# Four tiles and the samples gather first, and the last four tiles are dense

## The chip, the core and the metric

The kernel runs on one core of one Trainium2 chip. The metric is the device time in microseconds (us) of one execution. The version before takes 3297.21 us (median of 3 runs, 3287.35 to 3303.12).

## The reference

One layer of a decoder trunk is computed for a prompt of 1024 positions (eight tiles of 128) and for eight samples of four positions (32 rows, called the samples, tile NT = 8 in the code). Both use the same weights.

```python
ada = silu(c) @ W_ada + b_ada                    # shift, scale, gate, twice
y   = token_mixers(x * (1 + sc1) + sh1)          # mLSTM, spatial gating, pooling, then @ W_o
x   = LN(ALPHA * x + g1 * y)
q   = (x * (1 + sc2) + sh2) @ W_pq               # PEER: 8 heads, two halves of 128
s   = q . keys                                   # 128 keys a half; top 16 of each half
idx, g = top 16 of the 256 sums of both halves, softmax
act = gelu(x2 . peer_u[idx]); out = sum(g * act * peer_v[idx])
x   = LN(ALPHA * x + g2 * out)
```

Each position so picks 8 x 16 = 128 of 16384 experts. Each expert has a row of 1024 floats in `peer_u` and one in `peer_v`.

## The kernel before

**Two ways for the experts.** A tile is either gathered or dense. A gathered tile fetches its 128 u rows and 128 v rows for each position by indirect DMA on GpSimd's queue: 128 gathers of 128 rows for u and as many for v, 32 + 32 for the samples, 1088 in all for four tiles and the samples. VectorE multiplies each u gather with the tile (L1299), and TensorE adds each pair of v gathers with four small matmuls, each of them two records in the trace (L1356). The four dense tiles (512 positions) instead run through all 16384 experts, in 128 chunks of 128: 24 matmuls give a chunk's scores (`psd`, L1070), 12 matmuls for each of 256 output pieces add the results (`po`, L1177). Their gate matrix, mostly zeros, is built beforehand (`g_weights`, matmuls `pgm` at L1057) and stored in DRAM as G_d. For 32 of the 128 chunks `g_pre` computes the scores beforehand and stores them (`so`, L1092); this needs the split inputs of all four dense tiles (`g_x_split`).

**The stages.** `g_main` runs the projections and mixers of all tiles (`g_first`, `g_mixers`), then closes the projections' memory and opens that of the build. The generators beside it wait for keys in `ready`: `g_mixed` takes a group of tiles through W_o and the first layer norm (`g_mix`; z at L823), `g_routed` through the queries and the top-k (`g_route`; products at L880, scores at L890), `g_chosen` makes the final choice (`g_choice`, exponential at L917), `g_gates` builds the weights of a dense tile once it is chosen (first cast at L1030), and `g_gather` gathers. `run` orders their steps by estimated costs and by the weights in `PHASES`; a scheduler then puts the instructions of each engine into one order.

**Which tile does what.** Tiles 0, 1, 6, 7 and the samples are gathered, tiles 2 to 5 are dense. The groups [0, 1], [2, 3], [4, 5] and [6] are mixed and routed ahead of the dense stage. It starts once the build is closed. Tiles 7 and the samples are mixed and routed after that, in a memory scope "late" beside the dense stage (the key "late"), and g_main then closes that scope, opens another and goes on with the dense stage. One group streams all of w_o (8 transfers of 512 KB) and w_pq (16 of 512 KB).

**Memory that matters here.** The matmuls of mixing, routing, build and scores share a ring of five accumulation banks (tag "f"). `g_route` holds one score bank for two tiles and one product bank. The tags x (2 slots), h (8) and s (6) name slots in the front; `g_pre` uses two x slots for its inputs.

Of the kernel before, what the change touches and what calls it, by code (L numbers as in the profile page):

```python
# [17 lines left out]
P = 128  # L18
D = 1024
KD = D // P  # L20
NT = 8
# [21 lines left out]
    ("build", {"g_gates": 0.7, "g_even": 0.5, "g_odd": 0.5, "g_mixed": 0.5, "g_routed": 0.5, "g_gather": 0.7}),  # L43
    ("late", {"g_gather": 0.8}),
)
NROW = 6
MB = 2.78
GATHERED = (0, 1, 6, 7, NT)
DENSE = (2, 3, 4, 5)
PASSES = [0, 1], [2, 3, 4, 5, 6, 7, 8]  # L50
FRONT = [0, 1], [2, 3], [4, 5], [6]
BACK = [7, NT],
ND = len(DENSE) * P
# [24 lines left out]
def kernel(ctx: ExitStack, tc: tile.TileContext, A, O):  # L78
# [28 lines left out]
    def run(*parts):  # L107


        busy = [0.0, 0.0, 0.0]  # L110
        parts = [[0.0, i, g, None] for i, g in enumerate(parts)]
        now = 0.0
        late = False
        while parts:
            if "late" in ready and not late:
                late = True
# [167 lines left out]
    def load_consts():  # L284
        W["g"] = load("w_g", A["w_g"])
        for nm in ("bgT", "cmask", "cmask_s", "id4", "mhgT", "mneg_s", "keep_s", "bmask_s"):
            C[nm] = load(nm, A[nm])
        ones = C["ones"] = work("ones4", [4, P])
        V.memset(ones, 1.0)
        o1 = C["ones1"] = work("ones1", [P, 1])  # L290
        V.memset(o1, 1.0)
        V.memset(Cst, 0.0)

# [496 lines left out]
    def g_mix(ts):  # L790
# [4 lines left out]
        for t in ts:  # L795
            for h in range(2):
                yield from wait(("y", t, h))
            if t > 0:
                Y_[t] = slab("Y", (P, KD, P))
                nc.sync.dma_start(Y_[t][:, :, :ns[t]], ycat_d[t, :, :, :ns[t]])  # L800
        for e in range(2):
# [10 lines left out]
            for t in ts:  # L812
                if t not in z:
                    z[t] = slab("z")
                if t == ts[0] or t == NT:
                    g = bc_row("g1", G1 + e * 512, t, stream, 512)
                V.tensor_mul(z[t][:ns[t], e * 512:e * 512 + 512], py[t, e][:ns[t]], g[:ns[t], 0:512])
        for t in ts:
# [34 lines left out]
            if t == NT:  # L853
                x2T = X2[t] = slab("x2T", (P, KD, P))
                for e in range(2):
# [7 lines left out]
    def g_route(ts, early=False):  # L863

        ns = {t: NS if t == NT else P for t in ts}
        m = len(ts)
        for t in ts:
            top[t] = (work("TV", [P, 16, 16], F32, BUFS["t"]), work("TI", [P, 16, 16], U16, BUFS["t"]), keep("rt", [P, 2, 8, 16], bufs=6))
        for h in range(8):
# [3 lines left out]
            for p in range(2):  # L873
                c = 2 * h + p
                w = stream("wpq", (P, KD, P))
                nc.sync.dma_start(w, A["w_pq"][c])
                pq = bank("pqr", (P, 2, P))
                for i, t in enumerate(ts):
                    for k in range(KD):
                        mm(pq[:, i, :ns[t]], lhsT=w[:, k, :], rhs=X2[t][:, k, :ns[t]], start=(k == 0), stop=(k == KD - 1))  # L880
                qc = work("qc", (P, 2, P), F32, 2)
                for i, t in enumerate(ts):
                    if i and ns[t] == P:
                        continue
                    j = i + 1
                    while j < m and ns[ts[j]] == ns[t]:
                        j += 1
                    S.activation(qc[:, i:j, :ns[t]], pq[:, i:j, :ns[t]], AF.Copy)
                for i, t in enumerate(ts):
                    mm(sb[i // 2][:ns[t], i % 2, p, :], lhsT=qc[:, i, :ns[t]], rhs=kt[:, p, :], start=True, stop=True)  # L890
                yield 1.95 * m, 0, 0.58 * MB
# [205 lines left out]
    def g_dense(sc):  # L1097
# [126 lines left out]
        for j, op in enumerate(ops):  # L1224
# [27 lines left out]
            else:  # L1252
# [10 lines left out]
    V.tensor_copy(iota16, it32)  # L1263
    delta = keep("delta", [P, 32, 32], BF16)
    nc.gpsimd.memset(delta, 0.0)
    nc.gpsimd.affine_select(out=delta, in_=delta, pattern=[[1, 32], [-1, 32]], compare_op=ALU.not_equal, fill=1.0, base=0,
                            channel_multiplier=0)
# [8 lines left out]
    def u_items(t):  # L1276
# [29 lines left out]
        def finish():  # L1306
            if smp:
                s2 = keep("s2", [NS, P])
                for q in range(4):
# [16 lines left out]
    def v_items(t):  # L1326
# [7 lines left out]
        for j in range(nj):  # L1334
            for q in range(4):

                def step(j=j, q=q):
                    if j % 2 == 0 and q == 0:
                        ce_ = hold["c"] = cur["rows"].tile("cexp", [P, 2, 4, 32], F32, 2)
                        if smp:  # L1340
                            cv = cT_[:, 4 * j:4 * j + 8].rearrange("p (j q) -> p j q", q=4)
                            dv = delta[:, 4 * j:4 * j + 8, :].rearrange("p (j q) c -> p j q c", q=4)
                        else:
                            cv = cT_.rearrange("p (q j) -> p j q", q=4)[:, j:j + 2, :]
                            dv = delta[:, j:j + 2, :].unsqueeze(2).to_broadcast([P, 2, 4, 32])
                        V.tensor_tensor(out=ce_, in0=cv.unsqueeze(3).to_broadcast([P, 2, 4, 32]), in1=dv, op=ALU.mult)
# [118 lines left out]
    def g_main():  # L1465
# [14 lines left out]
        cur["build"].close()  # L1480
        cur["front"].close()
        cur["dense"] = Scope("dense")
        cur["fin"] = Scope("fin")
        cur["front"] = Scope("late")
        ready.add("late")
        BUFS["ws"] = 2
        BUFS["s"] = 5
        BUFS["t"] = 2
        dense = g_dense(cur["dense"])
        while "last" not in ready:  # L1490
            yield next(dense)
        flush(0)
        cur["front"].close()
        cur["fin"].close()
        cur["fin"] = Scope("fin2")
# [44 lines left out]
    def g_mixed():  # L1540
        yield from wait(("ada", 2))
        before = None
        for ts in FRONT:
            if before:
# [3 lines left out]
            before = ts  # L1548
        yield from wait("late")
        for ts in BACK:  # L1550
            yield from g_mix(ts)
            ready.add(("mixed", ts[0]))
            yield from wait(("routed", ts[-1]))

    def g_routed():
        for ts in FRONT + BACK:
            yield from wait(("mixed", ts[0]))
# [3 lines left out]
    def g_chosen():  # L1561
        for ts in list(FRONT) + list(BACK):
            yield from wait(("scored", ts[0]))
            yield from g_choice(ts, early=(ts[0] == 0))
            if ts == FRONT[-1]:
                ready.add("chosen")
        ready.add("last")

# [172 lines left out]
```

## Time and profile before

| | |
|---|---|
| median of 3 runs | 3297.21 us |
| profiled execution | 3293.14 us, span 3291.4 us |
| mean granted TensorE clock | 0.903 |
| PE busy | 2878.7 us (87%) |
| VectorE busy | 2206.4 us (67%) |
| ScalarE busy | 1019.0 us (31%) |
| GpSimd busy | 1323.3 us (40%) |
| DMA moved | 979.03 MB, mean 297 GB/s |

The span runs from the first to the last instruction. PE is TensorE's matmul row; its busy time is modelled and includes overlap. The granted clock is a share of 2.4 GHz, so 0.5 is the 1.2 GHz level. The dense stage runs in about the last half of the span.

### The profile page before, as it was taken

How to read it: one execution, taken by the hardware profiler on the slowest of the kernel's cores; microseconds unless marked ns; L12 is line 12 of the kernel's file. 1: busy time of each engine (PE TensorE's matmuls, PEld its weight loads, DVE VectorE, ACT ScalarE, POOL GpSimd, SP SyncE). 2: the span in 40 equal slices, each digit the busy share in tenths (PEclk: the TensorE clock that was granted, in tenths of full speed). 3: DMA queues.
4: the chain of work that ended last, by engine and by line, in shares of the span. 5: the costliest groups of instructions: out<-in, count | busy, mean ns of one | idle time of the engine just before them, and what ended most of it. 6: DMA issues, size and time to landing. Idle time of an engine off the chain costs nothing.

```text
span 3291.4 us, 45024 instructions
## 1 busy us (share of the span) xinstructions
PE 2878.7 (87%) x16366; PEld 1477.0 (45%) x16366; DVE 2206.4 (67%) x5761; ACT 1019.0 (31%) x1654; POOL 1323.3 (40%) x1096
## 2 busy tenths in 40 slices
PE   6878993587976899997788699999999999999996
PEld 3447942334654566444342464433444443333331
DVE  2443998777788877655445678766777776555546
ACT  3413243111021444456561124232323322222220
POOL 0000366545444533432233410544555554455544
PEclk8988996688978899996559799999999999999997
DMA  8743898889898888777578864999999999999986
GB/s 296 249 172 134 293 350 297 294 308 325 317 345 304 298 292 302 261 286 274 206 257 310 311 209 156 343 331 328 364 354 356 352 354 346 344 353 354 351 314 208
DMA packets 376498, 979.03 MB, mean 297 GB/s; under 512 B 37477, under 2 KB 116452, under 8 KB 372172
## 3 DMA queue, kind: packets, MB, share of 16 engines
q0 software_dynamic: 156672, 570.49, 47.8%
q1 hardware_dynamic: 219604, 405.67, 35.5%
q8 instruction: 128, 2.10, 0.3%
q14 instruction: 94, 0.77, 0.1%
HBM read 907.07 MB, written 69.02 MB: 297 GB/s over the span
## 4 chain that ended last, share of the span: by engine, by line
PE 57%; DMA 11%; DVE 6%; issue 4%; ACT 2%; POOL 1%; SPq 0%; POOLq 0%; DVEq 0%; ACTq 0%
PE psd L1070 17%; PE po L1177 16%; PE acc L1356 7%; PE pgm L1057 6%; DMA row<-in_peer_v,iT 6%; PE pqr L880 5%; DMA row<-in_peer_u,ii 3%; PE py L809 2%; POOL row L1272 1%; DVE row L1299 1%; ACT ab L1050 1%; DMA wo<-in_w_o 1%; PE ps L890 1%; DMA e<-x_d 1%; PE pvp L279 1%
## 5 line engine op out<-in xcount | busy, mean ns | idle before, releaser
L1272 POOL DMA_INDIRECT row<-in_peer_u,ii x544 | 672.4, 1236 | 1036.4 <-DVE ii L1295 316.0
L1272 POOL DMA_INDIRECT row<-in_peer_v,iT x544 | 647.6, 1190 | 875.0 <-PE acc L1356 494.8
L1299 DVE SCALAR_TENSOR_TENSOR row<-row,x2u 128x1024 f32<-128x1024 f32 x544 | 660.2, 1217 | 304.0 <-DMA row<-in_peer_u,ii 288.1
L1070 PE MATMUL psd<-xd,us 128*128 128x512 f16 x3072 | 709.5, 381 | 18.7 <-DMA xd<-xd_d 8.3
L1177 PE MATMUL po<-vs,coef 128*128 128x512 f16 x3072 | 701.3, 379 | 3.0 <-ACT coef L1167 1.7
L1070 PEld LDWEIGHTS <-us 128*128 128x128 f16 x3072 | 295.8, 99 | 430.9 <-issue 79.8
L1177 PEld LDWEIGHTS <-coef 128*128 128x128 f16 x3072 | 291.0, 98 | 430.3 <-issue 89.0
L1356 PE MATMUL acc<-row,cexp 128*32 128x512 f32 x2176 | 330.7, 662 | 127.4 <-DMA row<-in_peer_v,iT 127.1
L1057 PE MATMUL pgm<-ab 128*128 128x128 f16 x1024 | 265.4, 419 | 43.6 <-DVE ab L1047 23.1
L880 PE MATMUL pqr<-x2T,wpq 128*128 128x128 f32 (+1 forms) x2304 | 286.0, 283 | 1.9 <-DVE ns_s L707 0.7
L880 PEld LDWEIGHTS pqr<-x2T,wpq 128*128 128x128 f32 x2304 | 280.9, 199 | 10.9 <-DVE CT_s L712 1.5
L1160 ACT ACTIVATE act<-psd,scale 128x512 f32<-128x512 f32 x96 | 65.8, 685 | 513.5 <-PE psd L1070 503.7
L1057 PEld LDWEIGHTS <-ab 128*128 128x128 f16 x1024 | 149.7, 148 | 154.0 <-issue 40.4
L1186 DVE SCALAR_TENSOR_TENSOR acc<-po,scale,acc 128x512 f32<-128x512 f32 x248 | 182.9, 744 | 45.7 <-PE po L1177 40.4
L1162 DVE SCALAR_TENSOR_TENSOR act<-act,scale,g 128x512 f32<-128x512 f32 x128 | 95.7, 748 | 151.6 <-ACT act L1160 128.1
L1140 ACT ACTIVATE vs<-v 128x1024 f16<-128x1024 f32 x128 | 135.5, 1062 | 144.2 <-PE po L1177 123.0
L1060 ACT ACTIVATE gs<-pgm 128x256 f32<-128x256 f32 x256 | 139.8, 672 | 103.7 <-PE pgm L1057 96.8
L1141 DVE SCALAR_TENSOR_TENSOR vs<-v,vs 128x1024 f16<-128x1024 f32 x128 | 155.8, 1217 | 20.6 <-ACT vs L1140 19.7
L1356 PEld LDWEIGHTS acc<-row,cexp 128*32 128x32 f32 x2176 | 47.8, 112 | 259.3 <-DMA row<-in_peer_v,iT 148.3
L809 PE MATMUL py<-wo,Y 128*128 128x512 f32 (+1 forms) x288 | 141.2, 635 | 19.1 <-DMA wo<-in_w_o 10.6
L1050 ACT ACTIVATE ab<-ab,fl 128x128 f16<-128x128 f16 x192 | 118.8, 1034 | 84.5 <-DVE ab L1047 84.5
L279 PEld LDWEIGHTS <-w 128*128 128x128 f16 x2160 | 124.0, 100 | 26.4 <-issue 23.1
(346 smaller groups left out, 2923.2 us busy)
## 6 DMA issues: line engine op xcount, KB each, us to landing
v<-in_peer_v SPq DMA_DIRECT2D x128, 512.0 KB
u<-in_peer_uT SPq DMA_DIRECT2D x96, 512.0 KB
wpq<-in_w_pq SPq DMA_DIRECT2D x80, 512.0 KB
G_d<-gs SPq DMA_DIRECT2D x32, 1024.0 KB
g<-G_d SPq DMA_DIRECT2D x32, 1024.0 KB
wada<-in_w_ada SPq DMA_DIRECT2D x48, 512.0 KB
wf<-in_w_in SPq DMA_DIRECT2D x44, 512.0 KB
wo<-in_w_o SPq DMA_DIRECT2D x40, 512.0 KB
```

The source lines that it names most:

```text
L279: mm(out, lhsT=x if cs is None else y, rhs=y if cs is None else x, start=(i + k == 0), stop=(i == len(ps) - 1 and k == KD - 1))
L809: mm(py[t, e][:ns[t]], lhsT=Y_[t][:, k + j, :ns[t]], rhs=w[:, j, :], start=(k + j == 0), stop=(k + j == KD - 1))
L880: mm(pq[:, i, :ns[t]], lhsT=w[:, k, :], rhs=X2[t][:, k, :ns[t]], start=(k == 0), stop=(k == KD - 1))
L1050: S.activation(eq[:, :, j], eq[:, :, j], AF.Copy, scale=fl[:, b * BB + j:b * BB + j + 1])
L1057: mm(pg[:, j, :], lhsT=ab[:, 0, :, t4 + j], rhs=ab[:, 1 + e, :, t4 + j], start=(e == 0), stop=(e == 1))
L1070: mm(ps, lhsT=us[a][:, k, :], rhs=xd[:, :, b, k, :], start=(m == 0), stop=(m == 23))
L1141: V.scalar_tensor_tensor(out=vs[:, 1], in0=v, scalar=SV, in1=vs[:, 0], op0=ALU.mult, op1=ALU.subtract)
L1177: mm(po, lhsT=d[:, a, i * P:(i + 1) * P], rhs=vs[:, b, c % 2, :], start=(m == 0), stop=(m == 3 * GROUP - 1))
L1186: V.scalar_tensor_tensor(out=a, in0=po, scalar=scale[:, 3:4], in1=a, op0=ALU.mult, op1=ALU.add)
L1272: nc.gpsimd.indirect_dma_start(out=s[:], out_offset=None, in_=A[table], in_offset=bass.IndirectOffsetOnAxis(ap=idx, axis=0))
L1299: V.scalar_tensor_tensor(out=s, in0=s, scalar=1.0, in1=x2, op0=ALU.mult, op1=ALU.mult, accum_out=sv[:, k:k + 1])
L1356: return mm(pv[e][g:g + 32, :], lhsT=l, rhs=s[:, e * 512:e * 512 + 512], start=(j == 0), stop=(j == nj - 1), skip_group_check=True)
```

## The change

Gathered tiles become 0, 1, 2, 3 and the samples; tiles 4 to 7 are dense. There are four groups, [0, 1], [2, 3], [4, 5] and [6, 7, samples], all ahead of the dense stage; the scope "late", its second memory scope and its key are gone. Several buffers are laid out anew so that a group of three fits: the samples' Y, x2T and z take smaller or other slots, the query product has 288 columns with a single copy, `rt` has 8 buffers, the table `delta` is smaller and read with shifted columns, `ones` is a broadcast, and `s2` shares the slots of `cT_`.

```diff
-    ("late", {"g_gather": 0.8}),
+    ("dense", {"g_gather": 0.8}),
...
-GATHERED = (0, 1, 6, 7, NT)
-DENSE = (2, 3, 4, 5)
+GATHERED = (0, 1, 2, 3, NT)
+DENSE = (4, 5, 6, 7)
...
-FRONT = [0, 1], [2, 3], [4, 5], [6]
-BACK = [7, NT],
+GROUPS = [0, 1], [2, 3], [4, 5], [6, 7, NT]
...
-        ones = C["ones"] = work("ones4", [4, P])
-        V.memset(ones, 1.0)
...
+        C["ones"] = o1[0:4].to_broadcast([4, P])
...
-                Y_[t] = slab("Y", (P, KD, P))
+                Y_[t] = half("Y", (P, KD, NS)) if t == NT else slab("Y", (P, KD, P))
...
-                    z[t] = slab("z")
+                    z[t] = (xslab if t == NT else slab)("z")
...
-                x2T = X2[t] = slab("x2T", (P, KD, P))
+                x2T = X2[t] = half("x2T", (P, KD, NS))
...
-                pq = bank("pqr", (P, 2, P))
+                pq = bank("pqr", (P, 2 * P + NS))
...
+                S.activation(qc[:, :nq], pq[:, :nq], AF.Copy)
...
-    delta = keep("delta", [P, 32, 32], BF16)
+    delta = keep("delta", [P, 8, 64], BF16)
...
-                s2 = keep("s2", [NS, P])
+                s2 = keep("cT_", [P, P], bufs=2)[:NS]
...
+        ready.add("dense")
         cur["dense"] = Scope("dense")
-        cur["fin"] = Scope("fin")
-        cur["front"] = Scope("late")
-        ready.add("late")
-        BUFS["ws"] = 2
-        BUFS["s"] = 5
-        BUFS["t"] = 2
         dense = g_dense(cur["dense"])
-        while "last" not in ready:
-            yield next(dense)
-        flush(0)
-        cur["front"].close()
-        cur["fin"].close()
         cur["fin"] = Scope("fin2")
         load_rows()
         yield from dense
...
-        for ts in FRONT:
+        for ts in GROUPS:
             if before:
                 yield from wait(("routing", before[0]))
             yield from g_mix(ts)
             ready.add(("mixed", ts[0]))
             before = ts
-        yield from wait("late")
-        for ts in BACK:
-            yield from g_mix(ts)
-            ready.add(("mixed", ts[0]))
-            yield from wait(("routed", ts[-1]))
```

## Rows read from the trace of the kernel before

**Rows 1.** The page: its first line, and the engines' busy times.
```profile
span 3291.4 us, 45024 instructions
PE 2878.7 (87%) x16366; PEld 1477.0 (45%) x16366; DVE 2206.4 (67%) x5761; ACT 1019.0 (31%) x1654; POOL 1323.3 (40%) x1096
```

**Rows 2.** Stretches: length, busy us of each engine (instructions), clock, DMA share, GB/s.
```profile
1065.00:1500.00 435.00, 403.84 (x2242) 234.46 (x2243) 303.36 (x980) 199.70 (x345) 174.11 (x130) 0.96 0.81 288
1500.00:1705.00 205.00, 161.42 (x638) 84.05 (x637) 108.63 (x141) 134.66 (x245) 60.40 (x48) 0.51 0.65 233
1705.00:2060.00 355.00, 305.51 (x1585) 159.16 (x1583) 239.68 (x764) 86.03 (x144) 92.09 (x81) 0.92 0.74 252
...
2300.00:2750.00 450.00, 447.61 (x2194) 185.26 (x2193) 350.04 (x504) 137.03 (x170) 239.17 (x199) 1.00 0.97 356
2750.00:3210.00 460.00, 456.34 (x2359) 170.99 (x2358) 256.07 (x355) 122.89 (x156) 229.23 (x205) 1.00 0.95 342
```

**Rows 3.** Chain of waits: start us, length us, what.
```profile
2367.08 5.18 PE psd L1070 x24
```

**Rows 4.** Groups from 2750 to 3210 us: line, engine, tiles, xcount | busy us, mean ns.
```profile
L1177 PE MATMUL po<-vs,coef 128*128 128x512 f16 x963 | 220.4, 380 | 0.0
...
L1070 PE MATMUL psd<-xd,us 128*128 128x512 f16 x720 | 166.8, 380 | 0.0
L1356 PE MATMUL acc<-row,cexp 128*32 128x512 f32 x672 | 89.5, 605 | 3.7 <-DMA row<-in_peer_v,iT 3.4
```

**Rows 5.** Groups from 1705 to 2060 us.
```profile
L1177 PE MATMUL po<-vs,coef 128*128 128x512 f16 x408 | 95.1, 380 | 0.0
L1070 PE MATMUL psd<-xd,us 128*128 128x512 f16 x377 | 90.3, 389 | 0.0
L880 PE MATMUL pqr<-x2T,wpq 128*128 128x32 f32 (+1 forms) x512 | 61.2, 279 | 0.0
...
L809 PE MATMUL py<-wo,Y 128*128 128x512 f32 (+1 forms) x64 | 32.9, 649 | 5.2 <-DMA wo<-in_w_o 5.2
L1356 PE MATMUL acc<-row,cexp 128*32 128x512 f32 x136 | 30.0, 737 | 39.4 <-DMA row<-in_peer_v,iT 39.4
L890 PE MATMUL ps<-keys,qc 128*128 128x128 f32 (+1 forms) x64 | 11.9, 284 | 0.8 <-ACT qc L888 0.8
```

**Rows 6.** Line 678, the mixers' last output: ns min/median/max, first and last start us.
```profile
L678 DVE TENSOR_TENSOR out<-py,psT x8: 205/403/424, 210.9 to 1062.8; 128x256 f32<-128x256 f32 x7, 128x64 f32<-128x64 f32 x1
```

**Rows 7.** Line 823, z ahead of the layer norm, in stretches of 20 us (DVE).
```profile
900.00:920.00 20.00, 1.21 (x1) 0.74 0.96 351
1060.00:1080.00 20.00, 1.22 (x1) 0.54 1.02 396
```

**Rows 8.** Line 1030, the start of a dense tile's weights, in stretches (DVE).
```profile
1060.00:1080.00 20.00, 0.28 (x1) 0.54 1.02 396
...
1500.00:1520.00 20.00, 0.29 (x1) 0.50 0.87 336
1600.00:1620.00 20.00, 0.29 (x1) 0.50 0.66 232
```

**Rows 9.** Line 917, the exponential of a tile's choice, in stretches (ACT).
```profile
1220.00:1240.00 20.00, 1.59 (x2) 1.00 0.86 304
1340.00:1360.00 20.00, 0.13 (x1) 1.00 0.85 306
```

**Rows 10.** Line 1092, the stored scores: ns min/median/max, first and last start us.
```profile
L1092 ACT ACTIVATE so<-psd x32: 582/598/938, 1094.4 to 1494.2; 128x512 f32<-128x512 f32 x32
```

**Rows 11.** Chain of waits at the end.
```profile
3232.82 3.99 PE po L1177 x18
...
3287.01 1.27 DVE row L786
```

**Rows 12.** Groups from 1705 us to the end: the gathers on GpSimd's queue.
```profile
L1272 POOL DMA_INDIRECT row<-in_peer_v,iT x373 | 433.0, 1161 | 515.0 <-PE acc L1356 263.8 <-DVE row L1299 153.3 <-issue 61.4
L1272 POOL DMA_INDIRECT row<-in_peer_u,ii x227 | 275.4, 1213 | 345.2 <-PE acc L1356 153.9 <-DVE row L1299 120.0 <-issue 45.5
```

More of the change, by code (lines that the diff above doesn't have):

```diff
@@ L112, in run @@
         now = 0.0
-        late = False
+        dense = False
         while parts:
-            if "late" in ready and not late:
-                late = True
+            if "dense" in ready and not dense:
+                dense = True
                 now = max(busy)
@@ L866, in g_route @@
         m = len(ts)
+        nq = sum(ns.values())
         for t in ts:
-            top[t] = (work("TV", [P, 16, 16], F32, BUFS["t"]), work("TI", [P, 16, 16], U16, BUFS["t"]), keep("rt", [P, 2, 8, 16], bufs=6))
+            top[t] = (work("TV", [P, 16, 16], F32, BUFS["t"]), work("TI", [P, 16, 16], U16, BUFS["t"]), keep("rt", [P, 2, 8, 16], bufs=8))
         for h in range(8):
@@ L876, in g_route @@
                 nc.sync.dma_start(w, A["w_pq"][c])
-                pq = bank("pqr", (P, 2, P))
+                pq = bank("pqr", (P, 2 * P + NS))
                 for i, t in enumerate(ts):
                     for k in range(KD):
-                        mm(pq[:, i, :ns[t]], lhsT=w[:, k, :], rhs=X2[t][:, k, :ns[t]], start=(k == 0), stop=(k == KD - 1))
-                qc = work("qc", (P, 2, P), F32, 2)
+                        mm(pq[:, i * P:i * P + ns[t]], lhsT=w[:, k, :], rhs=X2[t][:, k, :ns[t]], start=(k == 0),
+                           stop=(k == KD - 1))
+                qc = work("qc", (P, 2 * P + NS), F32, 2)
+                S.activation(qc[:, :nq], pq[:, :nq], AF.Copy)
                 for i, t in enumerate(ts):
[L883 to L890, printed above, removed]
+                    mm(sb[i // 2][:ns[t], i % 2, p, :], lhsT=qc[:, i * P:i * P + ns[t]], rhs=kt[:, p, :], start=True, stop=True)
                 yield 1.95 * m, 0, 0.58 * MB
@@ L1263 @@
     V.tensor_copy(iota16, it32)
-    delta = keep("delta", [P, 32, 32], BF16)
+    delta = keep("delta", [P, 8, 64], BF16)
     nc.gpsimd.memset(delta, 0.0)
-    nc.gpsimd.affine_select(out=delta, in_=delta, pattern=[[1, 32], [-1, 32]], compare_op=ALU.not_equal, fill=1.0, base=0,
+    nc.gpsimd.affine_select(out=delta, in_=delta, pattern=[[1, 8], [-1, 64]], compare_op=ALU.not_equal, fill=1.0, base=32,
                             channel_multiplier=0)
@@ L1341, in step @@
                             cv = cT_[:, 4 * j:4 * j + 8].rearrange("p (j q) -> p j q", q=4)
-                            dv = delta[:, 4 * j:4 * j + 8, :].rearrange("p (j q) c -> p j q c", q=4)
+                            dv = delta[:, :, 32 - 4 * j:64 - 4 * j].rearrange("p (j q) c -> p j q c", q=4)
                         else:
                             cv = cT_.rearrange("p (q j) -> p j q", q=4)[:, j:j + 2, :]
-                            dv = delta[:, j:j + 2, :].unsqueeze(2).to_broadcast([P, 2, 4, 32])
+                            dv = delta[:, 0:2, 32 - j:64 - j].unsqueeze(2).to_broadcast([P, 2, 4, 32])
                         V.tensor_tensor(out=ce_, in0=cv.unsqueeze(3).to_broadcast([P, 2, 4, 32]), in1=dv, op=ALU.mult)
@@ L1548, in g_mixed @@
             before = ts
-        yield from wait("late")
-        for ts in BACK:
-            yield from g_mix(ts)
-            ready.add(("mixed", ts[0]))
-            yield from wait(("routed", ts[-1]))
     def g_routed():
-        for ts in FRONT + BACK:
+        for ts in GROUPS:
             yield from wait(("mixed", ts[0]))
@@ L1561, in g_chosen @@
     def g_chosen():
-        for ts in list(FRONT) + list(BACK):
+        for ts in GROUPS:
             yield from wait(("scored", ts[0]))
             yield from g_choice(ts, early=(ts[0] == 0))
-            if ts == FRONT[-1]:
-                ready.add("chosen")
-        ready.add("last")
+        ready.add("chosen")
     pend = []
```

## The prediction

> **What bounds the kernel now.** The page comes first [rows 1]: TensorE (PE) is busy for 87% of the span, VectorE (DVE) for 67%, so PE leads without being full. One execution took 3293.1 us for a span of 3291.4 us (1.7 us around it); the median of the three runs is 3297.2 us. The busy times by stretch, second, say where PE is not full [rows 2]: the build of the gate matrix ends at 1705 us, with a stretch from 1500 us on at half clock (0.51, the 1.2 GHz level); from 1705 to 2060 us the dense stage runs beside the mixing and routing of tiles 7 and NT; then PE is full to the end. DMA falls from 0.81 to 0.65 and 0.74 in the two middle stretches and is at 0.95 to 0.97 behind them.
>
> The third view, groups by line within a stretch, prices the dense stage. In the chain of waits, 24 of its matmuls take 5.18 us [rows 3], 0.216 us each. From 2750 to 3210 us there are 720 + 963 of them [rows 4]: 363.5 us of 460. The other 96.5 us go to 168 gathered v rows (672 accumulation records, four to a gather): 0.574 us each. So the dense stage is PE-bound at 0.216 us per matmul and 0.574 us per v gather. By that price the 377 + 408 matmuls and 34 v gathers from 1705 to 2060 us [rows 5] are worth 169.6 + 19.5 = 189 us, and that stretch took 355: **166 us are lost there**. The same groups show to what: 61.2 us of query products, 32.9 us of mixing and 11.9 us of scores, 106.0 us of PE, and some 60 us of waiting around them.
>
> The Trainium skill, Perfetto Trace Analysis, Identifying the Most-Contended Engine, holds matmul busy time to be a poor measure of headroom. Here it would mislead: PE's busy row in that stretch, 305.5 us [rows 2], leaves only 50 us to win, where the count of matmuls gives 166. By the busy row the sum below would end some 116 us later; I go by the count.
>
> **The change, part by part.**
>
> *Routing out of the dense stage.* The wait for "late" and the scopes around it go; tiles 7 and NT join tile 6 in one group ahead of the dense stage. Removed from the stage: 166 us, as above. What is late next is the dense stage itself, at PE's pace, with nothing left beside it but gathers.
>
> *The same work in the front.* It costs there what it issues: 106.0 us of PE. To this comes tile 6's own mixing, which now waits for all of its group. The last mixer output is written at 1062.8 us [rows 6], while tile 6 alone had its layer norm by 1060 to 1080 us [rows 7], so its 16.5 us (half of the 32.9) also fall behind 1065 us. Sum 122 us of PE. From 1065 to 1705 us PE is busy 404 + 161 of 640 us [rows 2], so 75 us are free, nearly all in the half-clock end where the chain is product, copy, next operand; I let 12 us of the free time hide something. Taken: **the dense stage starts 110 us later, at 1815 us**. Bounds: zero, if the free time and the wait-bound end absorb it (1705 us); and the whole build at the pace of its first half. The ends of that come from the next two items.
>
> *Order of the build.* Weights need a tile's routing. Before, the dense tiles were 2 to 5, and the first, third and fourth of them start in 1060:1080, 1500:1520 and 1600:1620 us [rows 8]; alone, a tile takes about 103 us (1500 to 1705 us, two tiles), and beside everything else the first two take 430 us. Now the first is tile 4, whose choice was made in 1220:1240 us [rows 9], so weights start about 155 us later. Four tiles alone from 1230 us would end at 1642 us; the first two at the shared pace and the last two alone, at 1230 + 430 + 206 = 1866 us; all four at the shared pace, at 2090 us. My 1815 us lies between, nearest to the middle one. From layer norm to choice the front takes about 275 us for tile 6 alone (1065 to 1340) and 320 us for tiles 4 and 5 (910 to 1230) [rows 7, 9]; at that, tile 6 is routed at about 1480 us, before its turn in the build.
>
> *The stored scores of 32 chunks.* They wait for the split of the last dense tile, now tile 7, so they begin about 70 us later than 1094 us [rows 10]. Their 768 matmuls then run beside routing and weights; that PE work is the same and is in the sum. The samples' z now sits in one of the two slots that also feed these chunks, until its rows are written: one chunk of 5.2 us to a few tens of us, hidden if routing has PE work meanwhile, and within my 12 us otherwise.
>
> *Banks.* The group of three holds three of five accumulation banks in mixing and in routing (two score banks and one product bank), where a single tile held two in routing. Weights and stored scores are left with two. Nothing in this trace has three; lower bound nothing, upper bound that the builds wait for the whole routing, which is the slow rival.
>
> *Transfers.* One round of w_o and w_pq fewer, 8 + 16 transfers of 512 KB on SP's queue; the queue issues the others in the same order. DMA is at 0.81 and less in the build, so I count nothing. POOL's queue keeps its 1088 gathers; only their tiles change. Tile 2 is routed early, so that u gathers don't stop at the end of tile 1's: at the 28 per 100 us of the build (POOL's 130 + 48 in 640 us) [rows 2], 110 us more hold 28 gathers more, half of them v: 14 x 0.574 = 8 us less in the dense stage.
>
> *The tail.* The last dense products stand in the chain at 3232.8 us and the last operation at 3287 us [rows 11]; the last 40 us are v gathers of tile 7 and the samples with a layer norm behind. 227 + 373 gathers were left at 1705 us [rows 12]. After, 572 are left at 1815 us; at 205 in 460 us [rows 2] they take 1284 us, while the dense stage needs 5376 x 0.216 + 359 x 0.574 = 1367 us (96 x 24 score and 256 x 12 output matmuls by the code). So the tail hides: **30 us off**, with the last output tile's own layer norm left. Bounds 0 and 40.
>
> *Small ones together.* The broadcast of ones, the smaller delta, the slots of s2 and the single copy of the query products change no operation of the dense stage; the copy becomes one instruction instead of two for the mixed group. Between -5 and +5 us; I take nothing.
>
> **Sum.** 3291.4 - 166 + 110 - 30 - 8 = 3197 us of span, 3199 us with what lies around; the median lies 4 us above the profiled execution, and I round up for the start of the dense stage, whose row loads now fall with its first transfers: **3205 us**.
>
> **Rivals.**
>
> *A: the front absorbs it.* For it: 75 us of free PE time, a stretch at half clock with routing to put into it, and weights of four tiles that take only 412 us alone. Against: PE is 93% busy from 1065 to 1500 us. The stage then starts at 1740 us: 3130 us.
>
> *B: the dense stage is bound by transfers.* If gathers do badly in the front (say 50 fewer), 622 are left; at 0.446 per us they take 1395 us, and the tail returns: 1815 + 1395 + 30 = 3240 us. For it: 356 GB/s at a DMA share of 0.97 from 2300 to 2750 us; against: 83 us of room above. The Trainium skill, DMA: Bandwidth & Descriptors, Specifications, puts the HBM limit of a core near 358 GB/s; the trace agrees (356), so the gathers could not speed up.
>
> *C: the move wins next to nothing.* Routing waits in the front as it did beside the dense stage: its full 166 us and tile 6's 16.5 us are added, the stage starts at 1888 us, 3278 us. For it: PE is 93% busy from 1065 to 1500 us; against: the last 205 us are not. The Trainium skill, Perfetto Trace Analysis, Optimization Strategy, holds that regimes with different bounds may gain from interleaving, which speaks against taking routing from beside the dense stage; in these rows both are PE work, so the trace bears the rule out only in part.
>
> *D: slower.* One mechanism: routing of the three-tile group ends late, because it waits for banks and for DVE's queue, and the weights of tiles 6 and 7 (206 us) can't start before. If routing time grew with tiles, 275 us for one would be some 620 for this group: from 1140 to 1760 us, the stage at 1966 us, 3356 us. For it: all four build tiles hang on this front, two on its last group. Against: two tiles together took 320 us, hardly more than one. It decides from a stage start of 1907 us on (the median of 3297 us), that is, from a choice of tile 6 at about 1701 us.
>
> **How the numbers follow.** Forecast 0.50, A 0.20, B 0.07, C 0.10, D 0.13. The forecast's own range is 3160 to 3255 us (stage start 1770 to 1865). Reaching into A and C, 3100 to 3295 us leaves out D and the low end of A, under 2 in 10. About 0.5% (16 us) is what a measurement of this kernel can tell from no change: faster 0.79 (the forecast, A, B and the lower part of C, 0.02), same 0.08 (the rest of C), slower 0.13 (D).
>
> **What would show it.** In the trace after: the dense activations start between 1770 and 1865 us; at once afterwards about 410 dense matmuls per 100 us, with no query products among them; DMA above 0.9 throughout; weights of tiles 6 and 7 still at the end of the build at half clock; u gathers without a gap in the build; last v gather before the last dense product. It is wrong if the stage starts after 1907 us, if gathers outlast the dense products by more than 40 us, or if the dense matmuls run slower than 0.216 us each with v gathers priced above.

## The result and the profile after

The changed kernel takes 3398.07 us (median of 4 runs, 3389.12 to 3400.78), where the kernel before took 3295.78 us in the same comparison: 1.0306 times as long, with an interval of 1.0274 to 1.0339. The prediction was 3205 us, faster. The sign is wrong.

The page after: its span, the engines' busy times, and what the DMA engines moved in each of 40 slices of 85 us.

```profile
span 3399.1 us, 44873 instructions
PE 2935.3 (86%) x16366; PEld 1491.1 (44%) x16366; DVE 2214.5 (65%) x5753; ACT 1010.0 (30%) x1618; POOL 1286.4 (38%) x1096
GB/s 291 245 182 120 314 339 301 282 330 326 309 317 292 330 333 292 252 270 273 233 279 248 221 300 173 128 216 326 352 361 348 362 318 337 341 346 341 319 311 68
```

The busy rows barely moved against [rows 1]: PE has the same 16366 matmuls. So the page does not say where 108 us of span went; the stretches do. Where the dense stage starts is read first, from the scores' activation (line, count, ns, first and last start), together with the stored scores (`so`) and the start of the four weights (`ix`):

```profile
L1154 ACT ACTIVATE act<-psd,scale x96: 670/687/689, 1992.9 to 3336.5; 128x512 f32<-128x512 f32 x96
L1086 ACT ACTIVATE so<-psd x32: 565/597/903, 1245.8 to 1749.6; 128x512 f32<-128x512 f32 x32
L1024 DVE CAST ix<-ptg x4: 269/286/292, 1336.3 to 1891.0; 128x128 int32<-128x128 f32 x4
```

The first and the third row of the kernel before (its second is [rows 10], from 1094.4 us):

```profile
L1160 ACT ACTIVATE act<-psd,scale x96: 667/687/688, 1711.0 to 3207.4; 128x512 f32<-128x512 f32 x96
L1030 DVE CAST ix<-ptg x4: 280/292/292, 1073.7 to 1612.0; 128x128 int32<-128x128 f32 x4
```

So the dense stage starts 282 us later, where 110 were predicted; the stored scores start 151 us later and the first weights 263 us later.

The stretches after, with the columns of [rows 2]:

```profile
1065.00:1325.00 260.00, 206.50 (x1211) 121.50 (x1211) 172.80 (x710) 45.76 (x79) 120.56 (x109) 0.86 0.90 324
1325.00:1750.00 425.00, 367.55 (x1911) 203.21 (x1910) 306.94 (x1019) 151.36 (x255) 187.83 (x143) 0.89 0.75 259
1750.00:1985.00 235.00, 198.17 (x813) 103.15 (x812) 123.67 (x154) 161.67 (x297) 67.82 (x57) 0.52 0.68 245
1985.00:2060.00 75.00, 75.00 (x340) 31.39 (x339) 52.12 (x73) 23.25 (x31) 11.56 (x8) 0.97 0.87 300
2060.00:2230.00 170.00, 170.00 (x791) 76.62 (x789) 93.08 (x112) 58.01 (x72) 1.88 (x2) 1.00 0.45 144
2300.00:2690.00 390.00, 390.00 (x1883) 159.37 (x1882) 299.89 (x435) 115.59 (x144) 201.61 (x169) 1.00 0.96 348
```

From 1065 to 1985 us PE is busy 206.50 + 367.55 + 198.17 = 772.2 of 920 us, 0.84. Before it was 565.3 of 640, 0.88 [rows 2]. PE got 207 us more to do and 73 us more of idling: nothing was absorbed. The accumulations of v gathers say most about the idling (columns as in [rows 4], 1065 to 1985 us):

```profile
L1351 PE MATMUL acc<-row,cexp 128*32 128x512 f32 x632 | 121.4, 820 | 77.2 <-DMA row<-in_peer_v,iT 77.2
```

Of the 147.8 us that PE idles in the front, 77.2 us end when a v gather lands; before it was 13.7 of 74.7 us, with 376 of these records (the row stands further below). The first 260 us hold no weights at all, and ACT, which copies their products, is busy for 46 us there. Then the weights of two tiles take 1325 to 1790 us at the shared pace, and those of the other two take the rest alone, at half clock.

The dense stage itself behaves as foreseen. From 2060 us on it is pure, and the chain of waits is an unbroken run of groups of 24 matmuls in 5.18 us, as in [rows 3]:

```profile
2061.98 5.18 PE psd L1064 x24
2067.16 5.18 PE po L1171 x24
2072.34 5.18 PE psd L1064 x24
```

It shows one new thing: GpSimd's queue stands from 2064 to 2229 us. The waits (engine, line and what it waited for: us in all, times, longest) and GpSimd's timeline there:

```profile
POOL row L1267 <- PE acc L1351: 168.5, 2, 164.7
```
```profile
2063.38 0.94 POOL L1267 DMA_INDIRECT row<-in_peer_v,iT  x1 [25.55 <-ACT vs L1134]
2228.99 0.94 POOL L1267 DMA_INDIRECT row<-in_peer_v,iT  x1 [164.67 <-PE acc L1351]
```

The next gather needs a buffer that an accumulation on PE frees, and PE runs 785 dense matmuls first. PE loses nothing by it then; the gathers are only shifted back. The stage takes 3399 - 1985 = 1414 us, 172 less than the 1586 us (1705 to 3291 us) before. The loss is in the front alone: +280 - 172 = +108 us.

### The profile page after: what moved, and what is told of

Read it like the earlier page. It is cut to its first block, busy times and chain, and to the rows that moved or that the text cites. A ratio compares the mean times of both kernels' runs of the same rounds, so it can differ in the third digit from the quotient of the medians.

```text
span 3399.1 us, 44873 instructions
## 1 busy us (share of the span) xinstructions
PE 2935.3 (86%) x16366; PEld 1491.1 (44%) x16366; DVE 2214.5 (65%) x5753; ACT 1010.0 (30%) x1618; POOL 1286.4 (38%) x1096
## 4 chain that ended last, share of the span: by engine, by line
PE 42%; DMA 3%; DVE 2%; issue 2%; ACT 1%; POOL 1%; POOLq 0%; ACTq 0%; DVEq 0%
PE po L1171 17%; PE psd L1064 14%; PE acc L1351 6%; PE pgm L1051 4%; DMA row<-in_peer_v,iT 3%; ACT ab L1044 1%; POOL row L1267 1%; ACT gs L1054 0%; DVE st L779 0%; DVE ab L1040 0%; DVE acc L784 0%; DVE acc L783 0%; DVE ab L1039 0%; DVE acc L1194 0%; DVE acc L1195 0%
## 5 line engine op out<-in xcount | busy, mean ns | idle before, releaser
L1267 POOL DMA_INDIRECT row<-in_peer_u,ii x544 | 663.3, 1219 | 965.2 <-DVE ii L1290 316.3
L1267 POOL DMA_INDIRECT row<-in_peer_v,iT x544 | 620.9, 1141 | 1030.3 <-PE acc L1351 670.8
L1064 PE MATMUL psd<-xd,us 128*128 128x512 f16 x3072 | 722.8, 387 | 29.4 <-ACT us L1081 24.0
L1351 PE MATMUL acc<-row,cexp 128*32 128x512 f32 x2176 | 364.2, 688 | 155.7 <-DMA row<-in_peer_v,iT 155.5
L1051 PE MATMUL pgm<-ab 128*128 128x128 f16 x1024 | 258.4, 421 | 36.2 <-DVE ab L1041 19.2
L1135 DVE SCALAR_TENSOR_TENSOR vs<-v,vs 128x1024 f16<-128x1024 f32 x128 | 156.1, 1220 | 53.8 <-ACT vs L1134 53.5
L1118 DVE SCALAR_TENSOR_TENSOR us<-u,us 128x1024 f16<-128x1024 f32 x96 | 117.4, 1223 | 33.8 <-ACT us L1117 28.3
```

Source lines behind the costliest of these rows:

```text
L1051: mm(pg[:, j, :], lhsT=ab[:, 0, :, t4 + j], rhs=ab[:, 1 + e, :, t4 + j], start=(e == 0), stop=(e == 1))
L1064: mm(ps, lhsT=us[a][:, k, :], rhs=xd[:, :, b, k, :], start=(m == 0), stop=(m == 23))
L1135: V.scalar_tensor_tensor(out=vs[:, 1], in0=v, scalar=SV, in1=vs[:, 0], op0=ALU.mult, op1=ALU.subtract)
L1267: nc.gpsimd.indirect_dma_start(out=s[:], out_offset=None, in_=A[table], in_offset=bass.IndirectOffsetOnAxis(ap=idx, axis=0))
L1351: return mm(pv[e][g:g + 32, :], lhsT=l, rhs=s[:, e * 512:e * 512 + 512], start=(j == 0), stop=(j == nj - 1), skip_group_check=True)
```

## The experiments

Two theories stood against each other at first. **Late supply**: the front is longer because its first weights and its stored scores come later, since tiles 4 to 7 and not 2 to 5 feed them. **Added work**: it is longer because the routing of tile 7 and the samples costs more there than 110 us, PE having no usable free time. A third was that the group of three holds too many accumulation banks. The runs on the kernel after all keep its new buffer layout; no run takes that alone.

**The old tile assignment, all else as after.**

```diff
-GATHERED = (0, 1, 2, 3, NT)
-DENSE = (4, 5, 6, 7)
+GATHERED = (0, 1, 6, 7, NT)
+DENSE = (2, 3, 4, 5)
```

> The changed kernel with one part undone: tiles 2 to 5 are dense again and tiles 6 and 7 gather, while all routing stays ahead of the dense stage in the same four groups. In the changed kernel the first dense tile's weights start at 1325 us and the dense stage at 1985 us. Theory T (the build starves: the weights and the stored scores wait for the routing and the split of tiles 4 to 7, which come late): weights start near 1075 us as before, the dense stage at 1780 to 1850 us, the time is 3200 to 3290 us. Rival U (routing three tiles beside the build slows the build, by banks and PE's queue, whatever tile is dense): the dense stage starts at 1930 us or later, 3340 us or more. A third outcome is possible under T: the gathers of tile 6 now start late, so that gathers end after the dense products and add up to 60 us at the end.

Measured: 3328.58 us, 1.0112 [1.0071, 1.0154] of before. The same three rows:

```profile
L1154 ACT ACTIVATE act<-psd,scale x96: 668/687/688, 1890.1 to 3253.9; 128x512 f32<-128x512 f32 x96
L1086 ACT ACTIVATE so<-psd x32: 538/597/887, 1087.5 to 1674.5; 128x512 f32<-128x512 f32 x32
L1024 DVE CAST ix<-ptg x4: 260/291/292, 1102.7 to 1795.8; 128x128 int32<-128x128 f32 x4
```

Stored scores and weights are back to within 7 and 29 us of before, and 103 of the 282 us go. The other 179 us stay with supplies as early as before. The start lies between the two that had been expected (1780 to 1850 us, and 1930 us or later), and so does the time: both theories hold a part.

**Both supplies early, with the tiles of after.** The weights are built from the gates of tiles 0 to 3, and the split inputs of the stored scores are taken from tiles 2 and 3, twice each, so the output is that of other gates and inputs; counts and shapes stay.

```diff
-            yield from wait(("routed", t))
-            yield from g_weights(i, t)
+            yield from wait(("routed", i))
+            yield from g_weights(i, i)
...
-            if t in DENSE:
-                yield from g_x_split(DENSE.index(t), t)
+            if t in (2, 3):
+                for i in (2 * t - 4, 2 * t - 3):
+                    yield from g_x_split(i, t)
+            if t in DENSE:
+                pass
...
-        for t in DENSE:
+        for t in (2, 3):
             yield from wait(("split", t))
```

> The changed kernel with both supplies of the build early: the four weight builds use the choices of tiles 0 to 3, and the stored scores use the split inputs of tiles 2 and 3 (each twice), so that neither waits for tiles 4 to 7; the dense tiles get other tiles' numbers, the amount of work is the same. Undoing the tile assignment moved the first dense activation from 1993 to 1890 us, early weights alone only to 1960 us. Theory T (two late supplies, weights and stored scores together, cost what the assignment cost): stored scores start near 1090 us, weights near 1100 us, first dense activation 1870 to 1910 us, the time 3300 to 3345 us. Rival G (the assignment cost time through the order of the gathers, not through supplies): first dense activation after 1940 us, 3350 us or more.

Measured: 3334.68 us (one run).

```profile
L1157 ACT ACTIVATE act<-psd,scale x96: 668/687/689, 1877.0 to 3267.6; 128x512 f32<-128x512 f32 x96
L1089 ACT ACTIVATE so<-psd x32: 564/597/934, 1051.4 to 1654.9; 128x512 f32<-128x512 f32 x32
```

With the tiles of after kept, early supplies give 116 us (1992.9 to 1877.0 us), somewhat more than the old assignment gives; they are also somewhat earlier than there (1051.4 us, and 1041.5 us for the first weights). The rival was the order of the gathers, with a stage start after 1940 us. So the supply is enough to explain what the assignment costs, 103 to 116 us. What fills the time shows in the accumulations of v gathers from 1065 to 1870 us:

```profile
L1354 PE MATMUL acc<-row,cexp 128*32 128x512 f32 x512 | 92.4, 760 | 33.7 <-DMA row<-in_peer_v,iT 33.7
```

PE waits 33.7 us for their transfers here, 77.2 us in the kernel after, though both gather the same tiles.

**Early weights alone**, the first half of that edit; the weights are those of other tiles' gates.

```diff
+            yield from wait(("routed", i))
+            yield from g_weights(i, i)
```

> The changed kernel, but the gate matrices of the four dense tiles are built from the choices of tiles 0 to 3, which come early (so the dense tiles get other tiles' gates). All routing, all weights and all other work are still done; only the wait of the weights for tiles 4 to 7 is gone. Theory T: the first weights start at 1070 to 1110 us instead of 1325 and the dense stage at 1850 us or earlier, 3270 us or less; the stored scores (done at 1755 us in the changed kernel) become the last to end. Rival U: the weights start early but are slowed, and the dense stage still starts after 1930 us, 3340 us or more.

Measured: 3358.18 us (one run).

```profile
L1154 ACT ACTIVATE act<-psd,scale x96: 667/687/687, 1959.7 to 3290.0; 128x512 f32<-128x512 f32 x96
L1086 ACT ACTIVATE so<-psd x32: 572/597/958, 1287.9 to 1763.3; 128x512 f32<-128x512 f32 x32
```

The stage starts 33 us earlier, where 1850 us or earlier was expected if late supply was the whole cause. Weights that start at 1102.7 us are worth only a third of the supply's part. PE still idles 71.3 us ahead of v accumulations in this front (1065 to 1955 us). The run above, which adds early stored scores to this edit, starts its stage another 83 us earlier.

**No group of three.**

```diff
-GROUPS = [0, 1], [2, 3], [4, 5], [6, 7, NT]
+GROUPS = [0, 1], [2, 3], [4, 5], [6, 7], [NT]
```

> The changed kernel with its last group split in two, [6, 7] and then the samples alone: no group holds three of the five accumulation banks, at the price of one more stream of w_o and w_pq. Rival U (banks): the dense stage starts 60 us or more earlier than 1985 us, 3340 us or less. Theory T: it starts between 1955 and 2015 us, 3370 to 3430 us.

Measured: 3404.91 us (one run).

```profile
L1154 ACT ACTIVATE act<-psd,scale x96: 670/687/689, 1936.1 to 3340.7; 128x512 f32<-128x512 f32 x96
L1086 ACT ACTIVATE so<-psd x32: 565/597/895, 1190.8 to 1693.4; 128x512 f32<-128x512 f32 x32
```

The stage starts 57 us earlier, between what the two theories had (60 us or more, and at most 30), but its last score activation is 4 us later than after. The group of three is not what made the kernel slower. Whether its banks cost something in the front stays open: the stored scores begin 55 us earlier here too (1190.8 against 1245.8 us), so that the earlier start may be the supply again. And this version takes 61 us more from first to last score (1404.6 against 1343.6 us). Of that, 31 more v gathers left on GpSimd's queue at its start (336 against 305) are worth 31 x 0.574 = 18 us; the rest was not settled.

**Less PE work in the same routing.** The query products of tiles 6, 7 and the samples run one of their eight steps; seven eighths of these products are left out. The rest is the version with the old assignment.

```diff
+                    kd = 1 if NT in ts else KD
-                    for k in range(KD):
+                    for k in range(kd):
```

> The changed kernel with tiles 2 to 5 dense (first dense activation at 1890 us, against 1711 us in the kernel before), and with one of the eight accumulation steps of the query products for tiles 6, 7 and the samples, so that their choices are others; all loads, copies, top-k and choices stay. It takes some 70 us of TensorE time out of the front. Theory P (the routing moved into the front costs its TensorE time): the first dense activation comes 60 to 85 us earlier, 1805 to 1830 us, and the time falls by as much, 3245 to 3270 us. Rival W (it costs by its waits, its order and what it does to the other engines): 30 us earlier or less, 1860 us or later, 3300 us or more.

Measured: 3228.11 us (one run).

```profile
L1155 ACT ACTIVATE act<-psd,scale x96: 668/687/687, 1814.9 to 3144.4; 128x512 f32<-128x512 f32 x96
```

The front of the version with the old assignment and of this one, each up to its dense stage:

```profile
1065.00:1885.00 820.00, 709.56 (x3640) 410.83 (x3639) 530.98 (x1720) 353.85 (x625) 254.04 (x207) 0.81 0.67 238
```
```profile
1065.00:1810.00 745.00, 628.66 (x2918) 335.37 (x2917) 504.81 (x1666) 354.59 (x626) 230.63 (x181) 0.79 0.69 244
```

PE does 80.9 us less and the stage starts 75 us earlier, while PE idles 110.4 us in the one and 116.3 us in the other. Work taken out comes back nearly one for one; the idle time stays. ACT, which copies the weights' products, is busy as long in both (353.85 and 354.59 us), so the chain of product, copy and next operand does not set the end by its length alone. The time falls by 100 us, 25 more than the start: the stage is shorter too, 1329.5 us from first to last score against 1363.8, which was not settled.

**More PE work.** 48 stored chunks in place of 32, in the kernel after and in the kernel before.

```diff
-PRE = [4 * g + 3 for g in range(32)]
+PRE = sorted([4 * g + 3 for g in range(32)] + [8 * g + 1 for g in range(16)])
```

> The changed kernel with 48 instead of 32 chunks of scores stored ahead: 16 x 24 matmuls of 0.216 us, 83 us of TensorE, go from the dense stage to the front. If the front is full on TensorE (theory P), the first dense activation comes 75 to 95 us later (2070 to 2090 us) and the time stays within 15 us of 3398 us. If the front has TensorE time free behind its waits (theory W), the first dense activation comes less than 45 us later and the time falls by 35 us or more, to 3365 us or less.

> The kernel before with 48 instead of 32 stored chunks, to see whether its half-clock stretch from 1500 to 1705 us (161 us of TensorE busy in 205) takes 83 us more of TensorE work. If it takes it: the first dense activation stays within 40 us of 1711 us and the time falls by 40 us or more, to 3255 us or less, which would beat both kernels. If TensorE is in effect full there: 60 to 90 us later, and the time within 15 us of 3295 us.

Measured: 3409.89 us, 1.0349 [1.0317, 1.0381], and 3374.87 us, 1.0241 [1.0204, 1.0279]. Their fronts:

```profile
1065.00:2095.00 1030.00, 876.13 (x4432) 466.09 (x4429) 633.95 (x1918) 387.70 (x668) 413.95 (x338) 0.84 0.77 272
```
```profile
1065.00:1800.00 735.00, 657.50 (x3310) 359.27 (x3311) 453.12 (x1178) 363.32 (x624) 262.12 (x207) 0.88 0.77 274
```

In the kernel after, 104 us more on PE move the stage by 106 us (2099.4 against 1992.9 us); in the kernel before, 92 us more move it by 95 (1806.2 against 1711.0 us), and its 74.7 idle us become 77.5.

```profile
L1154 ACT ACTIVATE act<-psd,scale x80: 668/687/687, 2099.4 to 3336.8; 128x512 f32<-128x512 f32 x80
L1160 ACT ACTIVATE act<-psd,scale x80: 669/687/692, 1806.2 to 3252.8; 128x512 f32<-128x512 f32 x80
```

**The kernel before had no free time to give, either.** This is the run that answers the question of free time most directly. Its time is a miss: it was expected within 15 us of 3295 us, since the stage has 83 us less to do, and rises by 79 us. From first to last score the stage gives back only 50 us (1446.6 against 1496.4 us), and what follows the last score is 43 us longer (127 against 84 us).

**Tiles 3 to 6 dense**, once in the kernel after (five groups, all in the front), once in the kernel before.

```diff
+GATHERED = (0, 1, 2, 7, NT)
+DENSE = (3, 4, 5, 6)
+GROUPS = [0, 1], [2, 3], [4, 5], [6], [7, NT]
```

> The changed kernel with tiles 3 to 6 dense, tiles 0, 1, 2, 7 and the samples gathered, and five groups in the front, [0, 1], [2, 3], [4, 5], [6], [7, samples]. Theory T: the first weights (tile 3) start near 1080 us, the stored scores near 1100 us as in the kernel before, and the dense stage at 1780 to 1850 us; since tile 2 keeps the gathers going, 3190 to 3270 us. Rival U: as e1 if the size of the last group matters (1800 us), but it would then beat e1 by 100 us or more; under T the two start the dense stage within 40 us of each other.

> The kernel before with tiles 3 to 6 dense and tiles 0, 1, 2, 7 and the samples gathered; tiles 7 and the samples are still routed beside the dense stage. By the two causes found (late supplies of the build, and TensorE work added to it) neither is present here: the first weights start near 1070 us, the stored scores near 1100 us, the first dense activation 1700 to 1760 us. Tile 2 is chosen at about 1010 us, so that the u gathers don't stop between tile 1's and tile 6's. If gathers set the 45 us behind the last dense product in the kernel before, the time falls to 3250 to 3285 us; if not, it stays within 15 us of 3296 us.

Measured: 3353.14 us, 1.018 [1.0137, 1.0223], its stage from 1892.2 us; and 3345.93 us, 1.0155 [1.013, 1.018]. Both are misses: the first was expected to start the stage at 1780 to 1850 us, the second at 1700 to 1760 us with a time of 3250 to 3285 us, or within 15 us of 3296 us. Rows of the second:

```profile
L1160 ACT ACTIVATE act<-psd,scale x96: 670/687/688, 1749.8 to 3276.4; 128x512 f32<-128x512 f32 x96
L1092 ACT ACTIVATE so<-psd x32: 567/598/953, 1113.1 to 1519.2; 128x512 f32<-128x512 f32 x32
```

With the dense tiles one later, the kernel before starts its stage 39 us later, and the stage then takes 30 us more from first to last score (1526.6 against 1496.4 us). The later start goes with a later supply (the first weights at 1161.8 us, not 1073.7), as in the pairs above; no run separates the two here, and why the stage lengthens was not found.

**Fewer stored chunks**: 24 and 16 in the kernel before, and 16 in the version with the old assignment, to see whether the front's price can be paid back to the stage.

```diff
+PRE = [4 * g + 3 for g in range(32) if g % 4 < 3]
...
+PRE = [8 * g + 7 for g in range(16)]
```

> The kernel before with 24 instead of 32 stored chunks: 8 x 24 matmuls, 41 us of TensorE, go from the front to the dense stage. Theory P (the build stretch runs at a fixed share of TensorE, 0.88 in the kernel before, and each microsecond of TensorE work in it costs 1.13 us or more): the first dense activation comes 40 to 55 us earlier than 1711 us, and the time falls by 5 to 40 us, to 3255 to 3290 us, since 16 more stored chunks cost 80 us. Rival W: it comes less than 25 us earlier and the time rises by 15 us or more.

> The kernel before with 16 stored chunks: 83 us of TensorE out of the front. Theory P: first dense activation 80 to 110 us earlier (1600 to 1630 us), the time 3230 to 3290 us. The build can't end before its weights do, whose last two tiles take 205 us alone, so the gain per chunk may be smaller than for the first eight.

> The changed kernel with tiles 2 to 5 dense and 16 stored chunks: against the same kernel with 32 (first dense activation 1890 us, 3329 us), theory P says 80 to 110 us earlier (1780 to 1810 us) and a time of 3270 to 3320 us, the routing in the front then costing about what it costs beside the dense stage.

Measured: 3293.2 us, 0.9988 [0.9973, 1.0003]; 3350.35 us, 1.0163 [1.0144, 1.0181]; and 3461.84 us, 1.0495 [1.0468, 1.0522]. The stages start at 1656.3, 1631.0 and 1831.9 us, 55, 80 and 58 us earlier than with 32 chunks, with 46, 80 and 81 us less PE work in the front, and take 85, 154 and 197 us more from first to last score. Each chunk has 24 matmuls, 5.18 us in the stage: 41 us for 8, 83 us for 16. So the stage loses more than the matmuls moved into it, and nothing is won by moving scores either way. The times that the theory of a full front gave (at most 3290, 3290 and 3320 us) are all missed, the last by 142 us. What the rest is was not settled. No version that computes everything beats the kernel before by a measurable amount.

## Why the prediction was wrong

**The step that failed** is the front's: "From 1065 to 1705 us PE is busy 404 + 161 of 640 us [rows 2], so 75 us are free ... Taken: the dense stage starts 110 us later, at 1815 us". It is 282 us later by the score activations (1711.0 to 1992.9 us), 280 by the stretches. Two things were wrong in it: the price of the added work, in "It costs there what it issues" above all, which is 69 us of the miss, and the late supply, taken as nothing, which is some 100 us.

*The price of the added work: 179 us, not 110.* The work itself was counted well. The groups of the front on PE (columns as in [rows 4]), before from 1065 to 1705 us, then the version with the old assignment from 1065 to 1885 us:

```profile
L1070 PE MATMUL psd<-xd,us 128*128 128x512 f16 x770 | 180.1, 383 | 18.7 <-DMA xd<-xd_d 8.3 <-ACT us L1087 8.3 <-DVE us L1088 2.1
L880 PE MATMUL pqr<-x2T,wpq 128*128 128x128 f32 x608 | 74.3, 279 | 0.0
L1356 PE MATMUL acc<-row,cexp 128*32 128x512 f32 x376 | 61.1, 728 | 13.7 <-DMA row<-in_peer_v,iT 13.7
L890 PE MATMUL ps<-keys,qc 128*128 128x128 f32 x76 | 14.3, 292 | 0.7 <-ACT qc L888 0.7
```
```profile
L1064 PE MATMUL psd<-xd,us 128*128 128x512 f16 x772 | 195.8, 408 | 18.9 <-ACT us L1081 17.9 <-issue 1.0
L879 PE MATMUL pqr<-x2T,wpq 128*128 128x128 f32 (+1 forms) x1152 | 139.7, 282 | 0.6 <-DVE z L815 0.6
L1351 PE MATMUL acc<-row,cexp 128*32 128x512 f32 x426 | 75.0, 734 | 24.0 <-DMA row<-in_peer_v,iT 23.9 <-DVE z L821 0.2
L807 PE MATMUL py<-wo,Y 128*128 128x512 f32 (+1 forms) x72 | 37.9, 678 | 10.2 <-DMA wo<-in_w_o 9.6 <-DMA Y<-ycat_d 0.5 <-ACT gs L1054 0.2
L884 PE MATMUL ps<-keys,qc 128*128 128x128 f32 x144 | 24.8, 296 | 1.0 <-ACT qc L882 1.0
L857 PE MATMUL pt<-ident,z 32*128 32x32 f32 x8 | 1.0, 288 | 10.1 <-DVE z L848 10.1
```

Products +65.4, mixing +37.9 (the kernel before has none behind 1065 us), scores +10.5: 114 us, where 122 were predicted. But the longer front also carries more of what runs beside it: 50 more accumulation records of v gathers (+13.9 us), and stored scores that run 25 ns slower each (+15.7 us). With small groups PE is busy 144 us longer, and idle 110 - 75 = 35 us longer. Of these 35 us the rows name 31: PE waits 10.2 us in the mixing, nearly all of it for w_o, 10.1 us for VectorE's rows of the samples (L857), and 10.3 us more than before for v gathers.

So three things are in this part. The 12 us taken off for free time were not there. The waits of the routing were put at nothing in the front, while the same prediction had counted 60 us of them beside 106 us of PE in the dense stage. And the side work, 30 us, has no term. That the 75 idle us lie "nearly all in the half-clock end" is a wrong reading of [rows 2]: 31 of them lie before 1500 us and 44 behind it.

Six pairs of runs put a price on PE work in the front alone. The stage moved by 75 us for 81 us of it, 106 for 104, 95 for 92, and with fewer stored chunks by 55 for 46, 80 for 80 and 58 for 81: 0.7 to 1.2 us for each, around one for one. Where work was added (106 and 95 us), PE's idle time did not shrink: it grew by 6 and 3 us. Where work was taken out it changed by -8 to +23 us.

*Late supply: 103 to 116 us, taken as nothing.* "Weights start about 155 us later" and "begin about 70 us later" were on the page, and 1866 us was worked out as "the middle one" of the bounds; the sum then took the PE value, 1815 us, as if the later of the two did not decide. Even 1866 us would have left the forecast on the faster side, at 3256 us: the two also add up. With the weights late, PE's early front is 206.50 of 260 us busy, 0.79, and from 1065 to 1330 us it waits 37.8 us for the transfers of v gathers that it adds up. From the version with the old assignment to the kernel after, the front grows by 100 us (820 to 920 us), and the accumulations of v gathers account for it: 46.4 us more of busy time (75.0 to 121.4 us, 426 to 632 records) and 53.2 us more of waiting for their transfers (24.0 to 77.2 us). By these rows each of the 51 gathers more takes some 1.9 us in the front, and it saves 0.574 us in the stage. This is a sum over rows and not an experiment; whether the front is shorter when gathers stand back until the weights come was not run. Weights in fact started 263 us later, not 155: tile 4's choice stands at 1280 to 1300 us here, against 1220 to 1240 us before [rows 9]. The stored scores started 151 us later, not 70: the layer norms of the last group stand between 1160 and 1240 us.

*The stage: right in kind.* Removed 166, predicted with the tail and the gathers as 204 us; measured 172, and 150 in the version with the old assignment (1885 to 3321 us). Two terms were off. A v gather cost about 0.7 us instead of 0.574: the scores' and outputs' 5376 matmuls at 0.216 us are 1161 us, and from 1985 us to the last dense addition at 3366.7 us there are 1382 us with 1240 accumulation records, 310 gathers, (1382 - 1161) / 310 = 0.71 us. The excess is some 43 us; by the same count some 15 of them lie from 2230 to 2300 us, right behind the standing queue, where 14 gathers leave 23.6 us beside 215 dense matmuls. Against that, the front that lasted longer had done 54 v gathers more than the 359 counted as left, 54 x 0.574 = 31 us. The tail from the last dense addition is 32 us, before 48: 16 us saved, not 30.

In the terms of the sum: 3205 + 170 (stage at 1985, not 1815 us) + 24 (stage of 1414, not 1390 us) = 3399 us.

*The rivals.* D named the right sign and the wrong place. "It decides from a stage start of 1907 us on" held in effect: the start is 1985 us and the kernel is slower. But its mechanism, the choice of tile 6 at 1701 us or later, is not what happened: tile 6's choice stands at 1580 to 1600 us, and its weights start only at 1780 us, behind tiles 4 and 5. The choice was late against the prediction's 1480 us, but it was not what the weights waited for, and that D's start of 1966 us comes within 19 us of the measured one is luck. Its banks are no cause of the time (five groups: 3404.91 us). C's first sentence, "Routing waits in the front as it did beside the dense stage", is the nearest: 183 us in place of the 179 found. Had C's 183 us stood with the late supply's 103 to 116, the start would have come out at 1991 to 2004 us. That 183 comes so close to 179 is partly luck: C has 122 us of work and 60 of waiting, the trace 114 of work, 30 of side work and 35 of waiting. A and B fell: nothing was absorbed, and the last gathers end before the last dense products.

The Trainium skill, Perfetto Trace Analysis, Optimization Strategy, says that a kernel whose most-contended engine changes over time may gain from interleaving those regimes. Both regimes are PE work here, so the sentence does not decide this case; the runs go its way by little. In the version with the old assignment, which takes the routing from beside the dense stage, the front pays 180 us and the stage gives back 150.

The row that would have told the price stood in the prediction: the routing took 166 us beside the dense stage for 106 us of PE. No row said that its waits would vanish in a front that itself idles 75 of 640 us.

Of the signs named for "What would show it": the stage start, the DMA share above 0.9 throughout (0.45 from 2060 to 2230 us), the start bound of 1907 us, the price of a v gather and the u gathers without a gap (none from 1140 to 1220 us) failed; the pure stage (785 dense matmuls in 170 us, 462 per 100 where 410 were named), 0.216 us a dense matmul, the half clock at the build's end and the last gather ahead of the last dense product held.

## What to carry to other kernels

Price work that is moved into a mixed stretch at its whole busy time, take nothing off for that stretch's idle time, and carry its waits along at what they were where it ran before, until a row shows that they are covered. Before a stage is fed by other tiles, work out when its first input comes, as a term of its own, and where a sum of work and a chain of starts give different ends, take at least the later, not a value between. Ask also what the busiest engine will do until that input comes: here it was work that waited for transfers.

## What the runs showed of the hardware

The granted clock falls to its 1.2 GHz level at the end of each build although PE is far from still: 0.52 from 1750 to 1985 us with PE busy 198 of 235 us, as 0.51 with 161 of 205 us before [rows 2]. It returns to 0.97 in the first 75 us of the dense stage, in which PE is busy throughout. More routing in the front did not lift it: this end takes 205 us before and 235 us after. With 48 stored chunks in the kernel before, whose scores run until 1661.5 us, the stretch at this level is shorter, 135 us (0.50 from 1665 to 1800 us), but PE's idle time in the whole front is hardly other, 77.5 us.
